# Transposed activations taken through DRAM by one write and one read, and two weight groups opened side by side at the start of a stage

## The chip, the cores and the metric

The kernel runs on one core of one Trainium2 chip. The metric is the device time of one execution in microseconds. Three runs of the kernel before lie within 0.1 us of each other.

## The reference

x has 256 rows (frames) of 1024 columns. Two layers do the same four things to it:

```python
h = rmsnorm(x, ffn1_norm[i]);  x = x + 0.5 * swiglu(h, w_gate, w_up, w_down)
h = rmsnorm(x, mix_norm[i]);   q_s, k_s, v_s, q_m = split(h @ w_in[i])
x = x + concat([self_attention(q_s, k_s, v_s), memory_attention(q_m, mem)]) @ w_out[i]
h = rmsnorm(x, ffn2_norm[i]);  x = x + 0.5 * swiglu(h, w_gate, w_up, w_down)
```

swiglu(h) is (silu(h @ w_gate) * (h @ w_up)) @ w_down with an inner width of 2816. Self-attention is chunked with a position bias in layer 0 and differential with rotary embedding in layer 1. All is f32 in DRAM.

## The kernel before, in words

The 256 rows are two blocks of 128, tb = 0 and 1. The stages follow one another: FFN, mixer, FFN, FFN, mixer, FFN. An FFN first goes through 11 groups of 256 inner columns (tile gu, gate and up side by side, one PSUM bank of 512 columns for each tb), then through 11 blocks of w_down (tile acc, four banks: tb by column half hf). A mixer has five projections of 512 columns (tile pj), attention, and an output projection (acc as well); the first mixer makes the memory's keys and values (tile kv) before its projections.

f32 precision comes from three products for each product: a weight is split into hi and lo, the activation into xh and xl, and `dense` (L376 to L393) issues hi with xh, lo with xh and hi with xl, each a matmul over 512 columns. The activation is the stationary operand, the weights stream.

Weights come in chunks of 1 MB (tile raw, three buffers, loaded by SP in the order of `add_chunk`). ScalarE casts a chunk to hi in four pieces (L302), VectorE subtracts to lo in four pieces (L314); hi and lo have four buffers each, and a buffer comes free when the last matmul with its chunk is done. In gu one chunk is one group and one half c of the 1024 rows, 12 matmuls for each tb.

The activations must stand transposed. After a stage `finish` (L460) adds the four acc banks to x, half by half: A = (tb 0, hf 0), B = (0, 1), C = (1, 0), D = (1, 1). `prep_half` (L417) turns the half by four TensorE transposes into a PSUM bank (tile xtp, L396), VectorE multiplies by the gain (y, L427), ScalarE casts to xh (L430), VectorE subtracts to xl (L432), and ScalarE later squares x for the norm (junk, L441). There are five such norms between stages: 1 to the first mixer, 2 to the second FFN, 3 to the third FFN, 4 to the second mixer, 5 to the last FFN. Half hf 0 feeds c = 0 of the next stage's first matmuls, hf 1 feeds c = 1. At the end of an FFN's down part the last three blocks are done for one acc bank after another (SPLIT, L554), so that the halves come one after another. A stage opens with group 0 alone: tb 0 c 0, tb 0 c 1, tb 1 c 0, tb 1 c 1.

The inner activation h of a group is evacuated by `evac` (L482): ScalarE makes sil (L491), VectorE h (L494) and four 128x128 block transposes (hb, L503), SP writes hb to DRAM (hd, L508) and reads it back by four DMAs of 32 partitions (hr, L514), and it is split into ht.

The order of every engine's queue is set by a planner in the program, the class Flow: it keeps an estimated time for each engine, lets the steps of all threads become due by estimates (3.0 us for the write and 4.0 us for the read of hd), and emits each instruction when it is due. On the chip each engine then works its queue off in that order and waits at the head of it.

## Time and profile before

| | us |
|---|---|
| Time, median of 3 runs (lowest, highest) | 974.91 (974.86, 974.94) |
| The profiled execution | 975.12 |
| Its span, first to last instruction | 973.3 |
| TensorE busy in the span | 964.6 |
| VectorE busy | 675.7 |
| ScalarE busy | 542.4 |

The profiled execution has 1.8 us outside its span and is 0.2 us above the median. The granted clock is 1.00 throughout. The profile counts a matmul as busy from its start to its modelled end, 0.39 us for 512 columns, while the next one starts 0.227 us later; so TensorE's real state is read from the distance of the starts and from the waits named in the timeline, not from its busy share.

### The profile page before, as it was taken

To read this page: it belongs to the slowest core of one execution; us is meant where nothing else is said; L and a number is where in the kernel's file an instruction comes from. 1 tells how busy PE (TensorE), PEld (TensorE's weight loads), DVE (VectorE), ACT (ScalarE), POOL (GpSimd) and SP (SyncE) were. 2 spreads that over 40 slices of the span, in tenths; PEclk is the share of its full clock that TensorE was granted. 3 is DMA by queue.
4 is the path that set the end of the run, shared out by engine and by line. 5 is a ranking of instruction groups with operands and counts; after the bars stand their busy time and mean duration, and the time that the engine had idled before them with its cause. 6 is when DMAs were issued, how large, how long until landed. Compare 5 with 4: busy or idle time off the path is not lost.

```text
span 973.3 us, 13393 instructions
## 1 busy us (share of the span) xinstructions
PE 964.6 (99%) x4576; PEld 791.3 (81%) x4576; DVE 675.7 (69%) x1485; ACT 542.4 (56%) x1159; POOL 60.1 (6%) x65
## 2 busy tenths in 40 slices
PE   9999999999999999999999999999999999999998
PEld 7888888887777888888888888888787788888886
DVE  6776675887777866666476676644989886676641
ACT  6554544766685655445445555443677764555540
POOL 0000000022210000000000000000344100000000
PEclk9999999999999999999999999999999999999999
DMA  9989766475525567887648887764641369788641
GB/s 289 306 242 270 257 225 206 162 260 173 174 87 173 163 209 223 242 263 242 235 124 252 250 252 237 253 207 136 207 140 50 125 199 284 235 251 254 226 130 44
DMA packets 164447, 200.90 MB, mean 206 GB/s; under 512 B 9433, under 2 KB 140058, under 8 KB 164378
## 3 DMA queue, kind: packets, MB, share of 16 engines
q1 hardware_dynamic: 164378, 200.04, 65.5%
q8 instruction: 36, 0.59, 0.3%
q14 instruction: 33, 0.27, 0.1%
HBM read 187.42 MB, written 12.58 MB: 205 GB/s over the span
## 4 chain that ended last, share of the span: by engine, by line
PE 91%; DVE 5%; ACT 1%; DMA 1%; issue 0%; SPq 0%; ACTq 0%
PE gu L383 16%; PE gu L386 16%; PE gu L389 16%; PE acc L386 9%; PE acc L389 9%; PE acc L383 9%; PE pj L389 3%; PE pj L383 3%; PE pj L386 3%; DVE lo L314 2%; PE xtp L396 1%; PE S L983 1%; PE AV L1064 1%; PE kv L389 1%; PE kv L386 1%; PE kv L383 1%
## 5 line engine op out<-in xcount | busy, mean ns | idle before, releaser
L314 DVE TENSOR_TENSOR lo<-raw,hi 128x512 fp32r<-128x512 f32 x656 | 416.5, 684 | 161.5 <-ACT hi L302 161.3
L302 ACT CAST hi<-raw 128x512 fp32r<-128x512 f32 x656 | 365.4, 618 | 241.3 <-PE gu L389 117.9
L389 PE MATMUL gu<-hi,xl 128*128 128x512 f32 x704 | 274.3, 390 | 0.0
L383 PE MATMUL gu<-hi,xh 128*128 128x512 f32 x704 | 274.1, 389 | 0.0
L386 PE MATMUL gu<-lo,xh 128*128 128x512 f32 x704 | 274.0, 389 | 0.0
L389 PEld LDWEIGHTS gu<-hi,xl 128*128 128x128 f32 x704 | 132.2, 188 | 27.5
L383 PEld LDWEIGHTS gu<-hi,xh 128*128 128x128 f32 x704 | 132.2, 188 | 27.3
L386 PEld LDWEIGHTS gu<-lo,xh 128*128 128x128 f32 x704 | 132.2, 188 | 27.2
L383 PE MATMUL acc<-hi,ht 128*128 128x512 f32 x352 | 137.7, 391 | 0.0
L386 PE MATMUL acc<-lo,ht 128*128 128x512 f32 x352 | 137.3, 390 | 0.2 <-DVE lo L314 0.2
L389 PE MATMUL acc<-hi,ht 128*128 128x512 f32 x352 | 137.4, 390 | 0.0
L386 PEld LDWEIGHTS acc<-lo,ht 128*128 128x128 f32 x352 | 66.1, 188 | 14.1 <-DVE lo L314 0.7
L389 PEld LDWEIGHTS acc<-hi,ht 128*128 128x128 f32 x352 | 66.1, 188 | 13.7
L383 PEld LDWEIGHTS acc<-hi,ht 128*128 128x128 f32 x352 | 66.1, 188 | 13.5
L523 DVE TENSOR_TENSOR ht<-hr,ht 128x512 fp32r<-128x512 f32 x44 | 30.3, 688 | 55.0 <-ACT ht L521 55.0
L521 ACT CAST ht<-hr 128x512 fp32r<-128x512 f32 x44 | 27.1, 617 | 69.5 <-DMA hr<-hd 69.5
L389 PE MATMUL pj<-hi,xl 128*128 128x512 f32 x160 | 64.6, 404 | 0.0
L386 PE MATMUL pj<-lo,xh 128*128 128x512 f32 x160 | 63.6, 398 | 0.0
L383 PE MATMUL pj<-hi,xh 128*128 128x512 f32 x160 | 63.6, 398 | 0.0
L491 ACT ACTIVATE sil<-gu,xr 128x256 f32<-128x256 f32 x88 | 41.4, 470 | 17.5 <-PE gu L389 17.5
L503 DVE STREAM_TRANSPOSE hb<-h 128x128 f32<-128x128 f32 x176 | 44.1, 289 | 1.2
L494 DVE SCALAR_TENSOR_TENSOR h<-gu,xr,sil 128x256 f32<-128x256 f32 x88 | 42.2, 480 | 1.6
(167 smaller groups left out, 806.5 us busy)
## 6 DMA issues: line engine op xcount, KB each, us to landing
raw<-in_ffn_w_down_dram SPq DMA_DIRECT2D x44, 1024.0 KB
raw<-in_ffn_w_gate_dram SPq DMA_DIRECT2D x86, 512.0 KB
raw<-in_ffn_w_up_dram SPq DMA_DIRECT2D x86, 512.0 KB
raw<-in_w_in_dram SPq DMA_DIRECT2D x32, 512.0 KB
hd<-hb SPq DMA_DIRECT2D x44, 256.0 KB
hr<-hd SPq DMA_DIRECT2D x176, 64.0 KB
raw<-in_w_out_dram SPq DMA_DIRECT2D x8, 1024.0 KB
raw<-in_w_mem_kv_dram SPq DMA_DIRECT2D x4, 1024.0 KB
```

The source lines that it names most:

```text
L302: nc.scalar.copy(out=c.hi[:, sl], in_=c.raw[:, sl])
L314: nc.vector.tensor_sub(c.lo[:, sl], c.raw[:, sl], c.hi.bitcast(F32)[:, sl])
L383: nc.tensor.matmul(out=ps, lhsT=xh, rhs=wh, start=start, stop=False)
L386: nc.tensor.matmul(out=ps, lhsT=xh, rhs=wl, start=False, stop=False)
L389: nc.tensor.matmul(out=ps, lhsT=xl, rhs=wh, start=False, stop=stop)
L396: nc.tensor.transpose(out=dst, in_=src, identity=flip if flipped else ident)
L491: nc.scalar.activation(sil, ps[tb][:, 0:256], AF.Silu, scale=xt.r[tb])
L494: nc.vector.scalar_tensor_tensor(out=h, in0=ps[tb][:, 256:512], scalar=xt.r[tb], in1=sil, op0=ALU.mult, op1=ALU.mult)
L503: nc.vector.transpose(out=hb[:, :, f, tb, :], in_=h[:, f * P:(f + 1) * P])
L521: nc.scalar.copy(out=hi, in_=src)
L523: nc.vector.tensor_sub(lo, src, hi.bitcast(F32))
L983: nc.tensor.matmul(out=ss[e][:, pr, :nk], lhsT=q[rows, pr, :], rhs=k[rows, pr, :], start=i == 0, stop=i == len(passes) - 1)
```

## The change

For a half marked `far`, prep_half makes no TensorE transposes: VectorE block-transposes x into xb, ScalarE's queue issues a DMA that writes xb to DRAM (xd) and then one that reads it back into 128 partitions with the blocks in place (xr); the gain is multiplied from xr, and the rest is as before. At norms 1, 3 and 4 all four halves are far, at norms 2 and 5 only C and D. The planner waits 4.2 us after the write and 5.6 us after the read.

The inner h goes by one block transpose of 256 columns for each tb, one write and one read of 128 partitions. Every FFN but the first opens with groups 0 and 1 side by side: tb 0 with c 0 of both, c 1 of both, then tb 1; the second mixer does so with projections 0 and 1. The weights are loaded in that order. The last down blocks before norms 3 and 4 are four in place of three.

```diff
@@ -336,15 +336,15 @@
     WO = (0, 1, 2, 3)
 
     def plan_ffn(l, nm, wg, wu, wd):
...
+        gu = [[None, None] for _ in range(NG)]
+        order = [(g, c) for g in range(NG) for c in range(2)]
+        if (l, nm) != (0, 1):
+            order[1:3] = order[2:0:-1]
+        for g, c in order:
+            pieces = 2 if len(chunks) < 2 else 1
+            a = cols4(wg[l], c, g * 256, 256, 0, pieces)
+            b = cols4(wu[l], c, g * 256, 256, 256, pieces)
+            gu[g][c] = add_chunk([q for ab in zip(a, b) for q in ab])
...
@@ -360,16 +360,16 @@
...
+        order = [(i, c) for i in range(len(WI)) for c in range(2)]
+        if l % 2 == 1:
+            order[1:3] = order[2:0:-1]
...
@@ -414,18 +414,41 @@
             self.rt = [None, None]
             self.done = [0, 0]
 
-    def prep_half(xt, tb, hf, gc, wait=0.0):
-        yield banks.has()
-        tp = bank("xtp")
-        for k in range(4):
-            t = turn(tp[:, k, :], xs[tb][:, hf * 512 + k * P:hf * 512 + (k + 1) * P])
-        yield t
-        yield g2.has()
-        y = g2.take([P, 4, P], F32, "y")
+    def prep_half(xt, tb, hf, gc, wait=0.0, far=False):
         ks = slice(hf * 4, hf * 4 + 4)
         g = gcol[:, gc + hf * 4:gc + hf * 4 + 4]
-        nc.vector.tensor_tensor(out=y, in0=tp, in1=g.unsqueeze(2).broadcast_to([P, 4, P]), op=ALU.mult)
-        banks.give()
+        if far:
+            yield g2.has(2)
+            xb = g2.take([P, 4, 4, 32], F32, "xb")
+            nc.vector.transpose(out=xb.rearrange("p b k j -> p k b j"),
+                                in_=xs[tb][:, hf * 512:(hf + 1) * 512].rearrange("p (k i b) -> p k b i", k=4, b=4))
+            yield flow.dve(512, 0.3)
+            d = dram.tile([4, 32, 4, P], F32, tag="hd", name="xd")
+            nc.scalar.dma_start(out=d.rearrange("a i b x -> (a i) (b x)"), in_=xb.rearrange("p b k j -> p (b k j)"))
+            flow.act(0, 0.25)
+            yield flow.now + 4.2
+            g2.give()
+            yield g2.has()
+            xr = g2.take([P, 4, P], F32, "xr")
+            nc.scalar.dma_start(out=xr, in_=d.rearrange("a i b x -> (i b) a x"))
+            flow.act(0, 0.25)
+            yield flow.now + 5.6
+            yield g2.has()
+            y = g2.take([P, 4, P], F32, "y")
+            nc.vector.tensor_tensor(out=y.rearrange("p k (a j) -> p k a j", a=4),
+                                    in0=xr.rearrange("p a (k j) -> p k a j", k=4),
+                                    in1=g.unsqueeze(2).unsqueeze(3).broadcast_to([P, 4, 4, 32]), op=ALU.mult)
+            g2.give()
+        else:
+            yield banks.has()
+            tp = bank("xtp")
+            for k in range(4):
+                t = turn(tp[:, k, :], xs[tb][:, hf * 512 + k * P:hf * 512 + (k + 1) * P])
+            yield t
+            yield g2.has()
+            y = g2.take([P, 4, P], F32, "y")
+            nc.vector.tensor_tensor(out=y, in0=tp, in1=g.unsqueeze(2).broadcast_to([P, 4, P]), op=ALU.mult)
+            banks.give()
         yield flow.dve(512)
         nc.scalar.copy(out=xt.h[tb][:, ks, :], in_=y)
@@ -472,7 +495,10 @@
...
-                yield from prep_half(xt, tb, hf, gc)
+                if far and hf == 0:
+                    flow.spawn(prep_half(xt, tb, hf, gc, far=True))
+                else:
+                    yield from prep_half(xt, tb, hf, gc, far=far)
@@ -499,24 +525,22 @@
                 if hb is None:
                     hb = g2.take([P, 4, 2, 2, 32], F32, "hb")
                 yield t
-                for f in range(2):
-                    nc.vector.transpose(out=hb[:, :, f, tb, :], in_=h[:, f * P:(f + 1) * P])
-                    t = flow.dve(128, 0.05)
+                nc.vector.transpose(out=hb[:, :, tb].rearrange("p b f j -> p f b j"),
+                                    in_=h.rearrange("p (f i b) -> p f b i", f=2, b=4))
+                t = flow.dve(256, 0.05)
                 g2.give()
+            yield t
             hd = dram.tile([4, 32, 4, P], F32, tag="hd", name="hd")
-            yield t
-            nc.sync.dma_start(out=hd.rearrange("a i b x -> (a i) (b x)"), in_=hb.rearrange("p b f t j -> p (b f t j)"))
+            nc.sync.dma_start(out=hd.rearrange("a i b x -> (a i) (b x)"), in_=hb.rearrange("p b t f j -> p (b t f j)"))
             yield flow.now + 3.0
             g2.give()
             yield g2.has()
-            hr = g2.take([P, 4, 2, 2, 32], F32, "hr")
-            for b in range(4):
-                nc.sync.dma_start(out=hr[32 * b:32 * b + 32].rearrange("p a f t j -> p a (f t j)"),
-                                  in_=hd[:, :, b, :].rearrange("a i x -> i a x"))
+            hr = g2.take([P, 4, P], F32, "hr")
+            nc.sync.dma_start(out=hr, in_=hd.rearrange("a i b x -> (i b) a x"))
             yield flow.now + 4.0
             yield g4.has()
             ht = g4.take([P, 2, 4, P], F32R, "ht")
-            src = hr.rearrange("p a f t j -> p (f t) a j")
+            src = hr.rearrange("p a (c j) -> p c a j", c=4)
             hi, lo = (ht[:, i].rearrange("p c (a j) -> p c a j", a=4) for i in range(2))
             nc.scalar.copy(out=hi, in_=src)
             yield flow.act(512)
@@ -525,20 +549,36 @@
...
-            order = [(tb, c) for tb in range(2) for c in range(2)] if g == 0 and (l, nm) != (0, 1) else \
-                    [(tb, c) for c in range(2) for tb in range(2)]
...
+        rest = 0
+        if (l, nm) != (0, 1):
+            grps = []
+            for tb in range(2):
+                for c in range(2):
+                    for g in range(2):
+                        if tb == c == 0:
+                            grps.append(open_group(g))
+                        run(grps[g], tb, c)
+            rest = 2
+        for g in range(rest, NG):
+            grp = open_group(g)
+            for c in range(2):
+                for tb in range(2):
+                    run(grp, tb, c)
...
-        SPLIT = NG - 3
+        SPLIT = NG - 4 if nm == 2 and gc_next is not None or l == 1 and nm == 1 else NG - 3
@@ -563,9 +603,14 @@
         if nm == 1:
             table_hint(AF.Exp)
         for tb in range(2):
-            flow.spawn(finish(acc, tb, nxt, gc_next, True))
+            flow.spawn(finish(acc, tb, nxt, gc_next, True, nxt is not None))
+            first = SPLIT if tb == 0 or SPLIT == NG - 3 else NG - 2
+            for c in range(SPLIT, first):
+                for k in range(2):
+                    for hf in range(2):
+                        down(c, k, tb, hf)
             for hf in range(2):
-                for c in range(SPLIT, NG):
+                for c in range(first, NG):
                     for k in range(2):
                         t = down(c, k, tb, hf)
                 acc.t[tb][hf] = t
@@ -846,16 +891,20 @@
...
+        def proj(*parts):
+            pss = []
             for tb in range(2):
                 for c in range(2):
...
+                    for n, (i, evac) in enumerate(parts):
+                        if tb == c == 0:
+                            flow.until(banks.has(2))
+                            pss.append([bank(f"pj{j}", (P, 512)) for j in range(2)])
...
@@ -1202,13 +1251,18 @@
                 memory_kv(ll)
         for c, tb in ((0, 0), (0, 1), (1, 0), (1, 1), (2, 0), (3, 0), (2, 1), (3, 1)):
             flow.spawn(unit(c, tb))
-        proj(0, qk_evac(0))
-        flow.until(g4.has(2))
-        take_v()
-        proj(1, v_evac)
-        proj(2, qk_evac(1))
-        proj(3, qk_evac(2))
-        proj(4, vq_evac)
+        if typ_a:
+            proj((0, qk_evac(0)))
+            flow.until(g4.has(2))
+            take_v()
+            proj((1, v_evac))
+        else:
+            flow.until(g4.has(3))
+            take_v()
+            proj((0, qk_evac(0)), (1, v_evac))
+        proj((2, qk_evac(1)))
+        proj((3, qk_evac(2)))
+        proj((4, vq_evac))
-            flow.spawn(finish(acc, tb, nxt, gc_next, False))
+            flow.spawn(finish(acc, tb, nxt, gc_next, False, tb == 1))
```

TensorE has 24 groups of four transposes of x before and 8 after; those left are the four at the program's start and A and B of norms 2 and 5.

ScalarE at norm 3, before, in the opening of the third FFN: hi are weights, xh_4484 is the activation of tb 1 (here its half D), gu_4932 the first group of tb 0.

```order
L302 CAST hi_4959<-raw_4820 128x512 x3
L430 CAST xh_4484<-y 128x512
L302 CAST hi_4959<-raw_4820 128x512
L491 ACTIVATE sil<-gu_4932,xr 128x256
L441 ACTIVATE junk,xss<-x_86 128x512
L302 CAST hi_5020<-raw_4942 128x512 x4
```

The cast of D stands ahead of the first sil. After, at the same place (xh_4383 is tb 0, xh_4384 is tb 1; gu_4818 and gu_4847 are groups 0 and 1 of tb 0):

```order
L302 CAST hi_4825<-raw_4770 128x512 x3
L427 DMA xd<-xb 128x512
L302 CAST hi_4825<-raw_4770 128x512
L453 CAST xh_4383<-y 128x512
L464 ACTIVATE junk,xss<-x_85 128x512
L433 DMA xr<-xd 128x4x128 x2
L517 ACTIVATE sil<-gu_4818,xr 128x256
L517 ACTIVATE sil<-gu_4847,xr 128x256
L453 CAST xh_4384<-y 128x512
L464 ACTIVATE junk,xss<-x_86 128x512
L453 CAST xh_4384<-y 128x512
```

The casts of C and D have moved behind both sil of tb 0, and two writes and two reads stand among the casts.

VectorE at norm 3, before, up to the first h (xl_4486 is tb 1):

```order
L427 TENSOR_TENSOR y<-xtp,gcol 128x512
L314 TENSOR_TENSOR lo_4925<-raw_4783,hi_4924 128x512 x2
L314 TENSOR_TENSOR lo_4960<-raw_4820,hi_4959 128x512 x2
L432 TENSOR_TENSOR xl_4486<-y,xh_4484 128x512
L314 TENSOR_TENSOR lo_4960<-raw_4820,hi_4959 128x512
L494 SCALAR_TENSOR_TENSOR h<-gu_4932,xr,sil 128x256
```

After, from the first h on (xl_4386 is tb 1):

```order
L520 SCALAR_TENSOR_TENSOR h<-gu_4818,xr,sil 128x256
L528 STREAM_TRANSPOSE hb<-h 128x2x4x32
L438 TENSOR_TENSOR y<-xr,gcol 128x512
L520 SCALAR_TENSOR_TENSOR h<-gu_4847,xr,sil 128x256
L438 TENSOR_TENSOR y<-xr,gcol 128x512
L455 TENSOR_TENSOR xl_4386<-y,xh_4384 128x512
```

The subtraction for C has moved behind the h of both groups and behind the products of C and D.

ScalarE at norm 4, before, in the opening of the second mixer (xh_6035 is tb 1, sq is the square of projection 0, tb 0):

```order
L302 CAST hi_6470<-raw_6334 128x512 x2
L302 CAST hi_6503<-raw_6378 128x512 x4
L430 CAST xh_6035<-y 128x512
L583 ACTIVATE sq<-pj_6485,xr 128x512
L441 ACTIVATE junk,xss<-x_86 128x512
L302 CAST hi_6566<-raw_6482 128x512 x4
```

And after (xh_5883 is tb 0, xh_5884 is tb 1; V is made from projection 1, tb 0):

```order
L453 CAST xh_5883<-y 128x512
L464 ACTIVATE junk,xss<-x_85 128x512
L433 DMA xr<-xd 128x4x128 x2
L628 ACTIVATE sq<-pj_6319,xr 128x512
L453 CAST xh_5884<-y 128x512
L979 ACTIVATE V_6317<-pj_6348,xr 128x512
L464 ACTIVATE junk,xss<-x_86 128x512
L453 CAST xh_5884<-y 128x512
```

Here the cast of C stands behind the sq of projection 0 alone, and ahead of V.

More of the change, by code (lines that the diff above doesn't have):

```diff
@@ L458, in __init__, with finish @@
             self.t = [[None, None], [None, None]]
-    def finish(acc, tb, xt, gc, half):
+    def finish(acc, tb, xt, gc, half, far):
         for hf in range(2):
@@ L526, in evac, with open_group, run @@
             hts[g], htt[g] = ht, t
-        for g, ids in enumerate(plan[l, nm, "gu"]):
+        def open_group(g):
             flow.until(banks.has(2))
-            ps = [bank(f"gu{tb}", (P, 512)) for tb in range(2)]
-            end = [None, None]
+            ps, end = [bank(f"gu{tb}", (P, 512)) for tb in range(2)], [None, None]
             flow.spawn(evac(g, ps, end))
-            order = [(tb, c) for tb in range(2) for c in range(2)] if g == 0 and (l, nm) != (0, 1) else \
-                    [(tb, c) for c in range(2) for tb in range(2)]
-            for tb, c in order:
-                for k in range(4):
-                    kk = 4 * c + k
-                    t = dense(ps[tb], xt.h[tb][:, kk, :], xt.l[tb][:, kk, :], lambda: xt.t[tb][kk], ids[c], k,
-                              lambda w: k4(w)[:, k, :], kk == 0, kk == KT - 1)
-                if c == 1:
-                    end[tb] = t
+            return g, ps, end
+        def run(grp, tb, c):
+            g, ps, end = grp
+            for k in range(4):
+                kk = 4 * c + k
+                t = dense(ps[tb], xt.h[tb][:, kk, :], xt.l[tb][:, kk, :], lambda: xt.t[tb][kk],
+                          plan[l, nm, "gu"][g][c], k, lambda w: k4(w)[:, k, :], kk == 0, kk == KT - 1)
+            if c == 1:
+                end[tb] = t
+        rest = 0
[13 more added lines that the diff above has]
+                    run(grp, tb, c)
         flow.until(banks.has(4))
```

42 lines of the change are left out of this document (14 added, 28 removed).

## The prediction

> **What bounds the kernel now.** I read the page's busy times and chain first.
>
> ```profile
> span 973.3 us, 13393 instructions
> ...
> PE 964.6 (99%) x4576; PEld 791.3 (81%) x4576; DVE 675.7 (69%) x1485; ACT 542.4 (56%) x1159; POOL 60.1 (6%) x65
> ...
> PE 91%; DVE 5%; ACT 1%; DMA 1%; issue 0%; SPq 0%; ACTq 0%
> ```
>
> TensorE bounds it: 91% of the chain is its own work, and VectorE and ScalarE have slack on the average. So an edit counts only if it takes instructions from TensorE or makes it wait. What TensorE's instructions cost stands in its timeline at norm 3, where one group of transposes sits between matmuls.
>
> ```profile
> 479.71 0.39 PE L383 MATMUL acc<-hi,ht 128*128 128x512 f32 x1
> ...
> 489.91 0.60 PE L396 MATMUL xtp<-ident,x 128*128 128x128 f32 x4
> ...
> 492.67 0.39 PE L386 MATMUL acc<-lo,ht 128*128 128x512 f32 x1
> ```
>
> From 479.71 to 489.91 there are 45 starts: 10.20 / 45 = 0.2267 us for a matmul. From 489.91 to 492.67 are 2.76 us with ten matmuls beside the group; ten take 2.27, so the group of four costs 0.49 us.
>
> **What is removed.** 16 of the 24 groups go (four halves at norms 1, 3, 4, two at 2 and 5): 16 x 0.49 = 7.84 us, all on the bound. Everything below asks how much of it waiting takes back.
>
> **What the handover is made of.** Call E the start of a stage's first matmul. Four blocks of 12 matmuls (tb 0: c 0 of both groups, c 1 of both) come before tb 1 in the changed opening, so C is wanted at Z = E + 48 x 0.2267 = E + 10.88, B at E + 5.44; the product with xl is the third, 0.45 later. The steps from x to xl, by operation (count | busy, mean ns | idle):
>
> ```profile
> L427 DVE TENSOR_TENSOR y<-xtp,gcol 128x512 f32<-128x512 f32 x24 | 16.5, 689 | 15.8 <-PE xtp L396 15.8
> L430 ACT CAST xh<-y 128x512 fp32r<-128x512 f32 x24 | 14.8, 618 | 33.6 <-DVE y L427 33.6
> L432 DVE TENSOR_TENSOR xl<-y,xh 128x512 fp32r<-128x512 f32 x24 | 16.5, 688 | 4.8 <-ACT xh L430 4.5
> L466 DVE SCALAR_TENSOR_TENSOR x<-acc,x 128x512 f32<-128x512 f32 x16 | 11.0, 690 | 20.0 <-PE acc L389 20.0
> ```
>
> And how closely engines follow each other, from the timeline at the opening of the third FFN and at two other places:
>
> ```profile
> 491.27 0.62 ACT L430 CAST xh<-y 128x512 fp32r<-128x512 f32 x1 [4.42 <-DVE y L427]
> 491.93 0.69 DVE L432 TENSOR_TENSOR xl<-y,xh 128x512 fp32r<-128x512 f32 x1 [0.69 <-ACT xh L430]
> ...
> 507.92 0.39 PE L389 MATMUL gu<-hi,xl 128*128 128x512 f32 x1
> ...
> 508.41 0.47 ACT L491 ACTIVATE sil<-gu,xr 128x256 f32<-128x256 f32 x1 [1.17 <-PE gu L389]
> ...
> 508.69 0.69 DVE L314 TENSOR_TENSOR lo<-raw,hi 128x512 fp32r<-128x512 f32 x1
> 508.78 0.62 ACT L441 ACTIVATE junk<-x 128x512 bf16<-128x512 f32 x1
> ...
> 509.30 0.48 DVE L494 SCALAR_TENSOR_TENSOR h<-gu,xr,sil 128x256 f32<-128x256 f32 x1
> 509.69 0.15 DVE L450 TENSOR_TENSOR sst<-xss 128x1 f32<-128x1 f32 x1
> ...
> 757.84 0.48 DVE L971 SCALAR_TENSOR_TENSOR oT<-otp,gcs,oT 128x256 fp32r<-128x256 f32 x1
> ...
> 758.37 0.49 PE L383 MATMUL acc<-hi,oT 128*128 128x512 f32 x1 [0.44 <-DVE oT L971]
> ```
>
> The last matmul of a tb starts at 507.92 and the slot after it at 508.15; sil starts at 508.41, so 0.26 after the slot. ScalarE's next instruction starts 0.37 after sil; VectorE's next starts 0.60 after one of 512 columns (508.69 to 509.30) and 0.39 after an h; xl starts 0.66 after its cast does; a stopped TensorE runs on 0.05 after VectorE's end (758.32 to 758.37) and its first matmul is 0.10 longer (0.49), 0.15 in all.
>
> **Added: a wait at norms 2, 3 and 5.** At norm 3 the cast of C stands behind the sil of group 1, tb 0, and that needs the last matmul before Z. At norms 2 and 5 ScalarE's order is the same. So however early C's data is there, sil starts at Z + 0.26, the cast runs from 0.63 to 1.25, and TensorE, which wants xl at Z + 0.45, must stand. VectorE then has h of group 1 at about Z + 0.78 (sil's end and a little), and its next at Z + 1.17. At norm 3 the product y of D stands there (0.60), so xl runs 1.77 to 2.46 and TensorE goes on at 2.61: 2.61 - 0.45 = 2.15 us. At norm 5 the block transpose hb of 256 columns stands there in place of y. Its row is not in the trace; the nearest:
>
> ```profile
> L503 DVE STREAM_TRANSPOSE hb<-h 128x128 f32<-128x128 f32 x176 | 44.1, 289 | 1.2
> L491 ACT ACTIVATE sil<-gu,xr 128x256 f32<-128x256 f32 x88 | 41.4, 470 | 17.5 <-PE gu L389 17.5
> L494 DVE SCALAR_TENSOR_TENSOR h<-gu,xr,sil 128x256 f32<-128x256 f32 x88 | 42.2, 480 | 1.6
> ```
>
> One of 128 takes 0.29, so the step is between 0.29 and 0.58; as for h (0.48, step 0.39) I take 0.35 to 0.4: 1.9 us. At norm 2 a short rotary step (0.15, like the sst above) comes too: 2.05. The lower bound of each is VectorE free: xl from 1.29 to 1.98, 1.7 us. The upper bound is a late read, below. Sum 6.1 us (5.1 at least). Nothing covers these: TensorE's queue has no other work ahead of tb 1.
>
> **Norm 4.** The cast of C stands behind the sq of projection 0, tb 0, only, and projection 0 ends 12 matmuls before Z.
>
> ```profile
> L583 ACT ACTIVATE sq<-pj,xr 128x512 f32<-128x512 f32 x12 | 8.2, 688 | 1.4 <-PE pj L389 1.4
> L586 DVE TENSOR_REDUCE hss<-sq 128x8 f32<-128x512 f32 x12 | 8.2, 680 | 1.4 <-ACT sq L583 1.4
> ```
>
> From E: 36 matmuls 8.16, sq from 8.42 to 9.11, on VectorE hss to about 9.8 and a short step, C's y from 10.0 to 10.7, cast to 11.35, xl to 12.1; wanted at 11.33, with the restart 0.9 us. It is 0 if y gets ahead of hss, and about 2 if D's steps get ahead. I take 0.9.
>
> **The way through DRAM.** No x goes that way before, but h does, in blocks of the same size; SP's issues (start, time of the issue) and the casts that take the data:
>
> ```profile
> 351.36 1.88 SPq L514 DMA_DIRECT2D hr<-hd  x4
> ...
> 358.71 0.62 ACT L521 CAST ht<-hr 128x512 fp32r<-128x512 f32 x1 [3.57 <-DMA hr<-hd]
> ...
> 518.15 0.51 SPq L270 DMA_DIRECT2D raw<-in_ffn_w_up_dram  x1
> 518.71 0.50 SPq L508 DMA_DIRECT2D hd<-hb  x1
> 524.09 2.43 SPq L514 DMA_DIRECT2D hr<-hd  x4
> ...
> 528.18 0.62 ACT L521 CAST ht<-hr 128x512 fp32r<-128x512 f32 x1 [1.96 <-DMA hr<-hd]
> ...
> 869.59 0.34 SPq L508 DMA_DIRECT2D hd<-hb  x1
> 871.79 1.39 SPq L514 DMA_DIRECT2D hr<-hd  x3
> ```
>
> A write takes 869.59 to 871.79 = 2.2 us, and 518.71 to 524.09 = 5.4 right behind a weight chunk. A read takes 524.09 to 528.18 = 4.1 and 351.36 to 358.71 = 7.35 at the outside. One read of 128 partitions in place of four of 32 is not in the trace; I take 4.1 to 5, near the shorter, since the issues of the four alone are 1.9 to 2.4 us of it. C's read is issued about E + 5 to E + 5.9 by ScalarE's order, so C lies in SBUF at E + 9.1 to E + 10.9 and needs y (0.69) by Z + 0.63: in time, by a little.
>
> The Trainium skill, in "DMA: Bandwidth & Descriptors" under "Issuing engines are not separate DMA queues", speaks against the queue of ScalarE's own: DMAs of all issuers share 16 engines and interleave, so only issuing time is saved. The write that took 5.4 us behind a weight chunk agrees that the load decides.
>
> **B at norms 3 and 4.** Before B's second step ScalarE has eight weight casts, a square and two DMA issues to do.
>
> ```profile
> 502.47 3.73 ACT L302 CAST hi<-raw 128x512 fp32r<-128x512 f32 x7
> ```
>
> That is 0.53 us a cast. From E - 1.1, where TensorE sets the buffers free, 8 x 0.53 + 0.63 + two issues (0.34 to 0.5 each, as SP's above) and the cast and xl of B end about E + 5.9, when B is wanted (E + 5.89). I take 0.1 each, 0.2 in sum (0 to 1).
>
> **Costed at nothing.** The 16 block transposes of x (estimate 0.7 to 1.2 us each, two to four times the 0.29 row) and the 88 of h in place of 176 (together some 13 us less of VectorE) lie on an engine 69% busy, in the slack ahead of each handover; without that cover each would cost about its time. One issue in place of four frees SP, which bounds nothing (0% of the chain). The 32 DMA issues on ScalarE wait at its head for the write; behind them are queued weight casts that mostly wait for TensorE's buffers. If that cover fails, lo comes late for TensorE by the write's excess, which is in the slower rival. Norm 1 has the memory's keys and values, 96 matmuls (21.8 us), in front of it: no gap. Four split blocks add no matmul.
>
> **Sum.** -7.84 + 6.1 + 0.9 + 0.2 = -0.64 us. The profiled execution took 975.12 (span 973.3 and 1.8 around it), 0.21 above the median; against the median 974.91 the sum gives 974.3 us.
>
> **Rivals.**
>
> *Faster.* The gaps are at their lower bound (5.1 + 0.9), and the second mixer, where TensorE waits already, gives its waits back because two projections now open it side by side.
>
> ```profile
> 686.00:786.00 100.00, 97.82 (x551) 77.56 (x550) 90.47 (x200) 68.87 (x191) 30.89 (x27) 1.00 0.46 149
> ```
>
> In these 100 us (the second mixer; busy time of TensorE, its loads, VectorE, ScalarE, GpSimd; granted clock; DMA share) TensorE lacks 2.2 us. The sum is -7.84 + 6.0 - 2.2 = -4.0: 970.9. For it: the removal is certain, and a more relaxed DVE helps there. Against it: VectorE is busy 90.47 of 100 there, so it may not be able to give.
>
> *Slower, by late reads.* C and D come at the outside time of the row, 7.35 us. The point from which it decides is a read over about 5.5 us at C. C then lands some 2 us later, and gaps become 3.9 at norms 3 and 4 and 2.9 at 2 and 5: 13.6 against 7.84 removed, with B's 0.2 about +6: 980.9. For it speaks the load just there:
>
> ```profile
> 510.00:520.00 10.00, 10.00 (x46) 8.29 (x45) 6.94 (x16) 5.51 (x11) 0.86 (x1) 1.00 0.92 286
> ```
>
> The DMA engines were 92% busy right after the opening of the third FFN, and the interleaved opening brings four chunks at that time. Against it: the reads of h meet the same load, and most took nearer to 4 us.
>
> In the Trainium skill, "TensorE: Matmul & The Clock Gate", "What's actually happening", an idle window of about 3.4 us halves TensorE's clock until it has been busy as long; by an estimate from that page, each such gap would lose 1.7 us more, some 984 in all. The granted clock is 1.00 throughout here, so no run yet shows it.
>
> *Slower, in the second mixer.* tb 0's first projection is done at E + 8.2 in place of E + 5.4, tb 1's at about 19 in place of 10.9, so attention starts 3 to 8 us later, and VectorE with its 90% can't catch up. If TensorE waits 3.2 us there, the sum is +2.6: 977.5. It decides from more wait than 2.6 us in that stage.
>
> *That it does not do what it says:* TensorE's order has the 16 groups gone, so that is no case of its own.
>
> **How the numbers follow.** The forecast, the waits taking back nearly all, has 0.43; faster 0.32; late reads 0.12; the second mixer 0.13. About 0.2% (1.95 us) is what a measurement of this kernel can tell from no change, so the forecast's own range, 972.9 to 976.5 by the bounds above, lies mostly in "same". From the cases: faster 0.34, same 0.42, slower 0.24. The range that leaves out no more than 2 in 10 goes from a little under the faster rival, 970.5, to above the mixer's one, 979.0; most of the late reads stay outside.
>
> **What would show it.** 8 groups xtp instead of 24 on TensorE; a stop of TensorE at its first product with xl of tb 1 near 2 us at norms 2, 3 and 5, released by VectorE's xl, whose cast began right behind a sil; about 0.9 at norm 4, none at norm 1. If those stops are under 1 us, the order argument is wrong; if ScalarE's idle before the cast or VectorE's before y ends by xr, the reads are late; if the second mixer's TensorE lacks more or less than 2.2 us per 100, a rival on it holds.

## The result and the profile after

The changed kernel takes 988.31 us (median of 4 runs, 986.29 to 990.69) against 974.88 for the kernel before on the same chip: a ratio of 1.0136 [1.0123, 1.0149], 13.4 us slower. The prediction said 974.3, with a range of 970.5 to 979.0. The profiled execution is the lowest of the four: 986.29 us, span 984.5. The page, its busy times and chain:

```profile
span 984.5 us, 12955 instructions
...
PE 963.2 (98%) x4512; PEld 786.0 (80%) x4512; DVE 701.3 (71%) x1413; ACT 543.1 (55%) x1159; POOL 61.0 (6%) x65
...
PE 86%; DMA 5%; DVE 5%; ACT 2%; POOL 0%; issue 0%; SPq 0%; ACTq 0%
PE gu L389 16%; PE gu L386 16%; PE gu L383 16%; PE acc L383 9%; PE acc L389 9%; PE acc L386 9%; DMA xd<-xb 3%; PE pj L383 2%; PE pj L389 2%; PE pj L386 2%; DMA xr<-xd 2%; PE S L1032 1%; PE AV L1113 1%; DVE lo L314 1%; PE ptp L396 1%; ACT hi L302 1%
```

DMA had 1% of the chain and has 5%: the write of xb and the read of xd stand on it. VectorE's work has grown, by 25.6 us. What TensorE waits for (line waited for: us in all, times, longest):

```profile
PE gu L383 <- ACT xh L453: 4.1, 3, 1.9
PE xtp L396 <- DMA x<-in_x_dram: 3.3, 1, 3.3
PE gu L389 <- DVE xl L455: 1.8, 4, 0.6
PE AV L1170 <- ACT PT L1046: 1.6, 1, 1.6
PE pj L383 <- ACT xh L453: 1.4, 1, 1.4
...
PE kmtp L396 <- DVE kmn L637: 1.1, 1, 1.1
PE qktp L396 <- DVE m L938: 0.9, 2, 0.6
PE pj L389 <- DVE xl L455: 0.5, 1, 0.5
```

The stops that were forecast are there (gu and pj, for xh and xl), and beside them one at the memory's keys (kmtp, norm 1) and some in the second mixer's attention (qktp, AV).

To put them in place I divide each profile at the first matmul of every stage and compare the stages' lengths with those of the kernel before. This table is worked out from the traces, in us of the profiled execution; "down" is the three down parts ahead of norms 1, 3 and 4, "mixer 1" includes the memory's keys and values, "rest" is the start, the first FFN's groups and the end. Medians are over all runs but two that stood far off, one of 1966 us in e2 and one of 1067 us in e5.

| kernel | down | mixer 1 | FFN 2 gu | FFN 3 gu | mixer 2 | FFN 4 gu | rest | span | median (before) |
|---|---|---|---|---|---|---|---|---|---|
| after | -4.3 | +0.3 | +1.7 | +4.5 | +4.3 | +3.3 | +1.4 | +11.2 | 988.31 (974.88) |
| e1 | -4.3 | +3.9 | +0.5 | +4.1 | +2.7 | +0.4 | +1.7 | +9.0 | 982.27 (975.32) |
| e2 | -0.1 | 0.0 | 0.0 | 0.0 | -1.9 | 0.0 | +2.2 | +0.3 | 973.86 (975.32) |
| e3 | 0.0 | 0.0 | 0.0 | 0.0 | -0.7 | 0.0 | -0.3 | -1.1 | 974.79 (975.32) |
| e4 | -1.4 | +2.1 | 0.0 | 0.0 | -0.7 | 0.0 | -0.1 | -0.2 | 975.30 (975.32) |
| e5 | -4.4 | +0.7 | +0.5 | +1.3 | +3.1 | +0.4 | +0.2 | +1.9 | 977.84 (975.23) |
| e6 | -4.4 | -0.9 | +0.6 | +1.2 | +3.1 | +0.7 | +0.2 | +0.4 | 975.62 (975.23) |
| e7 | -4.4 | +1.1 | +1.7 | +2.5 | +4.8 | +1.7 | +2.3 | +9.8 | 983.96 (975.23) |
| e8 | -2.0 | +1.8 | 0.0 | 0.0 | -1.5 | 0.0 | -0.2 | -1.9 | 973.39 (975.23) |
| e9 | -4.4 | -0.9 | +0.5 | +0.4 | +2.2 | +0.7 | +0.4 | -1.1 | 974.02 (974.89) |
| e10 | -0.1 | 0.0 | 0.0 | 0.0 | -1.8 | 0.0 | +0.4 | -1.5 | 973.58 (974.89) |
| e11 | -1.5 | +1.2 | 0.0 | 0.0 | -0.7 | 0.0 | +0.6 | -0.3 | 974.51 (974.89) |
| e12 | -1.0 | 0.0 | 0.0 | 0.0 | -1.8 | 0.0 | +0.5 | -2.3 | 972.70 (974.89) |

A stage that loses nothing would show minus 0.49 for each group of transposes that it no longer holds: one each in mixer 1's memory stage and in its output projection, one in FFN 2, one in FFN 3, two in mixer 2, one in FFN 4. "Rest" has nothing to do with the change after the first FFN's start: the first matmul comes at 8.6 to 11.0 us in these profiles, by when x arrives, and the first FFN's opening is the same code in all. e2 and e7 have besides 1.4 us of half speed there.

Where the time goes in the changed kernel is best seen at norm 3. ScalarE's rows there (start, length; ACTq are its DMA issues):

```profile
503.67 0.34 ACTq L427 DMA_DIRECT2D xd<-xb  x1
...
509.53 1.30 ACTq L433 DMA_DIRECT2D xr<-xd  x2
512.14 0.47 ACT L517 ACTIVATE sil<-gu,xr 128x256 f32<-128x256 f32 x1 [4.14 <-PE gu L389]
514.80 0.47 ACT L517 ACTIVATE sil<-gu,xr 128x256 f32<-128x256 f32 x1 [2.18 <-PE gu L389]
516.03 0.62 ACT L453 CAST xh<-y 128x512 fp32r<-128x512 f32 x1 [0.75 <-DVE y L438]
```

VectorE's product for C, in the same view:

```profile
515.30 0.69 DVE L438 TENSOR_TENSOR y<-xr,gcol 128x512 f32<-128x512 f32 x1 [1.49 <-DMA xr<-xd]
```

And TensorE:

```profile
514.38 0.39 PE L389 MATMUL gu<-hi,xl 128*128 128x512 f32 x1
516.70 0.50 PE L383 MATMUL gu<-hi,xh 128*128 128x512 f32 x1 [1.93 <-ACT xh L453]
517.04 0.40 PE L386 MATMUL gu<-lo,xh 128*128 128x512 f32 x1
517.64 0.80 PE L389 MATMUL gu<-hi,xl 128*128 128x512 f32 x1 [0.20 <-DVE xl L455]
518.24 0.63 PE L383 MATMUL gu<-hi,xh 128*128 128x512 f32 x1
518.66 0.63 PE L386 MATMUL gu<-lo,xh 128*128 128x512 f32 x1
```

C's write was issued at 503.67 and its read at 509.53, 5.9 us later; the read landed at 515.30, 5.8 us later. The sil of group 1 was at 514.80, so here both reasons meet: by the order alone the cast could have come at 515.17 (514.80 and 0.37), the data moved it to 516.03. TensorE stood 1.93 us. Then something that the sum did not hold: from 518.24 on the matmuls are 0.42 us apart in place of 0.227. The windows of that stretch (busy times; then granted clock, DMA share, GB/s) say why:

```profile
512.00:516.00 4.00, 2.76 (x13) 1.95 (x11) 1.82 (x4) 0.95 (x2) 0.00 (x0) 1.00 1.09 329
516.00:520.00 4.00, 3.10 (x8) 2.17 (x9) 2.94 (x7) 2.38 (x6) 0.55 (x1) 0.66 0.46 148
```

The granted clock was 0.66 in the four us behind the stop: TensorE ran at half speed for part of them. The DMA engines were full while C's read was under way.

At norm 2 C's data was early, and the order alone is seen. ScalarE, then TensorE:

```profile
332.25 0.47 ACT L517 ACTIVATE sil<-gu,xr 128x256 f32<-128x256 f32 x1 [2.18 <-PE gu L389]
332.62 0.61 ACT L453 CAST xh<-y 128x512 fp32r<-128x512 f32 x1
```

```profile
331.82 0.39 PE L389 MATMUL gu<-hi,xl 128*128 128x512 f32 x1
333.28 0.50 PE L383 MATMUL gu<-hi,xh 128*128 128x512 f32 x1 [1.07 <-ACT xh L453]
...
334.54 0.50 PE L389 MATMUL gu<-hi,xl 128*128 128x512 f32 x1 [0.52 <-DVE xl L455]
```

The sil starts, the cast follows 0.37 later, and TensorE's starts are 1.46 and (333.62 to 334.54) 0.92 apart in place of 0.23 each: 1.9 us in all, as the sum had it, with no half clock behind.

At norm 5 TensorE stops twice in the same way, and there half speed follows:

```profile
809.46 0.50 PE L383 MATMUL gu<-hi,xh 128*128 128x512 f32 x1 [1.07 <-ACT xh L453]
...
810.72 0.72 PE L389 MATMUL gu<-hi,xl 128*128 128x512 f32 x1 [0.53 <-DVE xl L455]
811.24 0.63 PE L383 MATMUL gu<-hi,xh 128*128 128x512 f32 x1
```

The windows tell the two places apart. I lay them so that one begins where the half speed does, first at norm 5, then at norm 2:

```profile
807.42:810.83 3.41, 1.81 (x8) 0.87 (x6) 2.44 (x6) 1.60 (x4) 0.00 (x0) 1.00 1.10 344
810.83:814.24 3.41, 3.41 (x9) 2.64 (x10) 1.38 (x4) 1.24 (x3) 0.56 (x1) 0.50 0.29 91
...
329.55:332.96 3.41, 2.66 (x12) 1.88 (x10) 2.13 (x6) 1.19 (x3) 0.00 (x0) 1.00 1.05 338
332.96:336.37 3.41, 2.56 (x10) 1.83 (x11) 3.05 (x9) 2.00 (x6) 0.00 (x0) 1.00 0.45 148
```

The half speed at norm 5 lasts from 810.83 to 814.24, 3.41 us at a clock of 0.50; at norm 3 it lasts as long, from 517.28. The two begin 293.55 us apart, 86 times 3.413, and the two of e1 below (from 210.07 and 520.69) 91 times. This fits windows of 3.413 us on a fixed grid. On that grid both stops of norm 5 lie in one window, while at norm 2 a border, 332.96, falls between them and each window keeps more of its work (2.66 and 2.56 us in place of 1.81).

### The profile page after: what moved, and what is told of

Same layout as the page of the kernel before. It is cut to its first block, busy times and chain, and to the rows that moved or that the text cites. A ratio compares the mean times of both kernels' runs of the same rounds, so it can differ in the third digit from the quotient of the medians.

```text
span 984.5 us, 12955 instructions
## 1 busy us (share of the span) xinstructions
PE 963.2 (98%) x4512; PEld 786.0 (80%) x4512; DVE 701.3 (71%) x1413; ACT 543.1 (55%) x1159; POOL 61.0 (6%) x65
## 4 chain that ended last, share of the span: by engine, by line
PE 86%; DMA 5%; DVE 5%; ACT 2%; POOL 0%; issue 0%; SPq 0%; ACTq 0%
PE gu L389 16%; PE gu L386 16%; PE gu L383 16%; PE acc L383 9%; PE acc L389 9%; PE acc L386 9%; DMA xd<-xb 3%; PE pj L383 2%; PE pj L389 2%; PE pj L386 2%; DMA xr<-xd 2%; PE S L1032 1%; PE AV L1113 1%; DVE lo L314 1%; PE ptp L396 1%; ACT hi L302 1%
## 5 line engine op out<-in xcount | busy, mean ns | idle before, releaser
L528 DVE STREAM_TRANSPOSE hb<-h 128x256 f32<-128x256 f32 x88 | 55.7, 632 | 1.2
```

The costliest lines, as they stand in the source:

```text
L528: nc.vector.transpose(out=hb[:, :, tb].rearrange("p b f j -> p f b j"), in_=h.rearrange("p (f i b) -> p f b i", f=2, b=4))
```

## The experiments

All times are medians; the ratio is that of the runs of one call with its 95% interval. Four theories are told apart: the **order** (C's cast behind the sil of group 1), the **data** (writes and reads under load are late), the **clock** (half speed behind a stop), and the **queue** (other work behind an engine that stands for the data).

**e1: the cast ahead of the sil.** In `evac`, tb 0 of group 1 in an opening:

```diff
                 yield end[tb]
+                if rest and g == 1 and tb == 0:
+                    yield lambda: xt.t[1][0] is not None
...
```

> The changed kernel, with one thing moved: at norms 2, 3 and 5 ScalarE's cast of C stands ahead of the sil of group 1, tb 0. Order theory (the stop before tb 1 comes from that sil): norm 2 falls from 1.9 to about 0.95 us and norm 5 from 2.2 to 0.85, by where y of C ends in the changed kernel's trace, and with the shorter stop the half clock behind norm 5 (1.6 us) goes: about 984.4 us against 988.3. Norm 3 stays, since there C's read lands only after the sil. Late-read theory (the data is what is late everywhere): all stops stay, 988.3.

Measured: 982.27 us, ratio 1.0063 [1.0043, 1.0082]. FFN 2 falls from +1.7 to +0.5, FFN 4 from +3.3 to +0.4 with its half clock gone, FFN 3 stays (+4.1): the order theory, as told, and at norm 3 the data theory. The median fell 6.0 us, more than the 3.9 expected, though this profile had a worse stop at the memory's keys than the changed kernel's. Its row, and two of the matmuls behind it, show the data and the queue at work at norm 1:

```profile
208.66 0.44 PE L396 MATMUL kmtp<-ident,kmn 128*128 128x128 f32 x2 [3.00 <-DVE kmn L638]
...
210.53 0.63 PE L386 MATMUL kv<-lo,memh 128*128 128x512 f32 x1
210.96 0.63 PE L389 MATMUL kv<-hi,meml 128*128 128x512 f32 x1
```

A stop of 3.0 us, and half speed behind it (0.43 us apart). VectorE in the same kernel:

```profile
207.23 0.69 DVE L438 TENSOR_TENSOR y<-xr,gcol 128x512 f32<-128x512 f32 x1 [2.08 <-DMA xr<-xd]
...
208.12 0.48 DVE L638 SCALAR_TENSOR_TENSOR kmn<-kv,mr,hf 128x256 f32<-128x256 f32 x1
```

VectorE stands 2.08 us at C's product for the read; kmn, the normalisation of the keys, is queued right behind, and TensorE needs it.

**e2: no x through DRAM.** Both `finish` calls get False for `far`; openings, split blocks and h stay.

```diff
-            flow.spawn(finish(acc, tb, nxt, gc_next, True, nxt is not None))
+            flow.spawn(finish(acc, tb, nxt, gc_next, True, False))
...
-            flow.spawn(finish(acc, tb, nxt, gc_next, False, tb == 1))
+            flow.spawn(finish(acc, tb, nxt, gc_next, False, False))
```

> The changed kernel with all transposes of x on TensorE again; openings side by side, four split blocks and the new way of h stay. If the way of x through DRAM makes the stops (14.5 us at the five norms in the profile of the changed kernel), they go and 7.8 us of transposes come back: about 981.7 us, with the 3.0 us lost in the second mixer and the 1.6 us at the start still there. If the openings or the new way of h make the stops: 988.3 + 7.8 = 996. If everything lost hangs on x through DRAM, mixer included: 977.

Measured: 973.86 us, ratio 0.9983 [0.9971, 0.9994]. Lower than every forecast: with the transposes back on TensorE (7.8 us of work) the kernel is 14.4 us below the changed one. All that is lost hangs on the way of x through DRAM, the second mixer included, which gains 1.9 us.

**e3: the new h alone**, in the kernel before.

```diff
-                for f in range(2):
-                    nc.vector.transpose(out=hb[:, :, f, tb, :], in_=h[:, f * P:(f + 1) * P])
+                nc.vector.transpose(out=hb[:, :, tb].rearrange("p b f j -> p f b j"),
...
-            for b in range(4):
-                nc.sync.dma_start(out=hr[32 * b:32 * b + 32].rearrange("p a f t j -> p a (f t j)"),
+            nc.sync.dma_start(out=hr, in_=hd.rearrange("a i b x -> (i b) a x"))
...
```

> The kernel before, with only the new way of h (one block transpose of 256 columns for each tb, one write, one read of 128 partitions). The prediction costed it at nothing: 974.9 within 1 us. Rival: the wider transposes and the single read delay weights or h, and part of the 13.4 us is theirs: 977 or more.

Measured: 974.79 us, ratio 0.9994 [0.9983, 1.0005]: no change in time, as costed. The profile has 0.75 us less in the second mixer.

**e4: the new h, and x through DRAM at norm 1 only**, old openings.

```diff
-            flow.spawn(finish(acc, tb, nxt, gc_next, True))
+            flow.spawn(finish(acc, tb, nxt, gc_next, True, l == 0 and nm == 1))
...
```

> The kernel before, with the new way of h and with x through DRAM at norm 1 alone (old openings, three split blocks). Four groups gone are 1.96 us. If the price there is the 1.2 us that the first mixer's memory keys wait in the changed kernel's profile: 974.1. If norm 1 is free: 972.9. If ScalarE's waits at the DMAs delay more: over 975.5.

Measured: 975.30 us, ratio 1.0001 [0.9990, 1.0011], between the 974.1 of the first case and the 975.5 of the last. The down part gives 1.4 (three groups) and the first mixer loses 2.1 where 0.49 should go. TensorE's waits:

```profile
PE kmtp L396 <- DVE kmn L637: 2.2, 2, 1.6
```

Norm 1 is not free, and the keys are the place.

**e5: nobody waits for the data.** e1, with the product from x itself, which leaves out the transposition:

```diff
-                                    in0=xr.rearrange("p a (k j) -> p k a j", k=4),
+                                    in0=xs[tb][:, hf * 512:(hf + 1) * 512].rearrange("p (a k j) -> p k a j", a=4, k=4),
```

> e1 with the gain multiplied from x itself instead of from what was read back: transposes, writes, reads and their order stay, only nobody waits for the data (this leaves out the transposition of x in 16 halves). Late-read theory for what is left after e1 (norm 1 where VectorE stands at C's y with the memory's keys queued behind it, norm 3 and norm 4 at C): these stops and the half clock after them go, only B's stop at norms 3 and 4 (0.7 each, xl behind four weight subtractions) stays: 976 to 978 against 982.3. If ScalarE's standing at the writes or the traffic is what costs: stays near 982.

Measured: 977.84 us, ratio 1.0029 [1.0015, 1.0043], 4.4 below e1 and in the band. FFN 3 falls from +4.1 to +1.3 and mixer 1 from +3.9 to +0.7: the data theory at norms 1 and 3. Mixer 2 does not fall (+3.1, of which 0.95 is half speed behind its AV stop that e1's profile does not have). In mixer 1 a stop of 1.6 at later keys is left, and it has another cause. ScalarE's casts of weights there, with the square for these keys queued behind them:

```profile
217.56 1.14 ACT L302 CAST hi<-raw 128x512 fp32r<-128x512 f32 x2 [2.74 <-DMA raw<-in_w_in_dram]
```

They wait 2.74 us for a weight chunk.

**e6: no DMA either.** e5 without the two `dma_start` of `prep_half`; it leaves out the transposition too.

```diff
-            nc.scalar.dma_start(out=d.rearrange("a i b x -> (a i) (b x)"), in_=xb.rearrange("p b k j -> p (b k j)"))
...
-            nc.scalar.dma_start(out=xr, in_=d.rearrange("a i b x -> (i b) a x"))
```

> e5 without the 32 DMAs (the block transposes stay; this leaves out the transposition of x in 16 halves and its way through DRAM). If waiting for the data was all: the same as e5 within 1 us. If ScalarE's standing at its queue's head for the writes, or the 8.4 MB of traffic, cost beside it: 2 us or more below e5.

Measured: 975.62 us, ratio 1.0007 [0.9998, 1.0016]: 2.2 below e5, just over the 2 us that was set for it, from only four runs of e5 between 976.4 and 980.0. The spans of the two profiles differ by 1.4 us, and the stages show it in mixer 1 (+0.7 to -0.9). The casts that stood for the weight chunk begin at 215.31 in place of 217.56, and the stop at the later keys is gone. SP issued those weights at 209.34 in place of 209.94, so about 0.6 us of it is from what came before, and the rest points to the DMA engines' load: from 192 to 208 their share is 0.66, then 0.75 here, and 1.01, then 1.07 in e5. That is for norm 1 alone. The more telling number is the level: with no transposes of x on TensorE and no DMA for it, the kernel is still no faster than before. The order of what is left, and VectorE's block transposes (e9), with the stops and half speed they bring, take all 7.8 us back.

**e7: idle matmuls in the stops.** The changed kernel, nine matmuls ahead of tb 1's first in each opening:

```diff
+        def fill(ps, xh, c):
+            for _ in range(9):
+                nc.tensor.matmul(out=ps, lhsT=xh, rhs=k4(c.hi)[:, 0, :], start=True, stop=True)
...
+                        if tb == 1 and c == g == 0:
+                            fill(grps[0][1][1], xt.h[0][:, 0, :], plan[l, nm, "gu"][0][0])
...
```

> The changed kernel with nine idle matmuls (9 x 0.227 = 2.0 us, into a bank that the next matmul starts afresh) on TensorE in the four stops before tb 1 at norms 2 to 5. They take the place of standing, so they cost about nothing there. Clock theory (the half clock behind norms 3 and 5 comes from the stop): it goes, 3.4 us in the profiled execution: 984 to 985 against 988.3. If the half clock has another cause, or its time is not on the end: 988.3 to 989.

Measured: 983.96 us, ratio 1.0088 [1.0066, 1.0110], 4.3 below the changed kernel with 8.2 us more of TensorE work (36 matmuls). FFN 3 falls from +4.5 to +2.5, FFN 4 from +3.3 to +1.7. The windows at norm 3 of this kernel, which hold the nine and what follows:

```profile
514.00:518.00 4.00, 4.00 (x19) 3.32 (x18) 2.74 (x6) 1.66 (x4) 0.00 (x0) 1.00 1.13 324
518.00:522.00 4.00, 4.00 (x19) 3.17 (x18) 2.05 (x7) 2.17 (x7) 0.55 (x1) 1.00 0.37 116
```

Granted clock 1.00 where the changed kernel had 0.66, and no half speed at norm 5 either: the clock theory holds. Work that does nothing made the kernel faster.

**e8: x through DRAM where the half has time**: `far` by half, A and B at norm 1, A at norms 3 and 4.

```diff
+            flow.spawn(finish(acc, tb, nxt, gc_next, True, (tb == 0, tb == 0 and l == 0 and nm == 1)))
...
+            flow.spawn(finish(acc, tb, nxt, gc_next, False, (False, False)))
...
```

> The changed kernel with x through DRAM only where the half has time: A and B at norm 1, A at norms 3 and 4; all else by TensorE as in e2. If the way through DRAM pays where nobody waits for it: four groups, 1.96 us, below e2: about 972. If it costs by its mere work on VectorE and ScalarE: 974 or more.

Measured: 973.39 us, ratio 0.9994 [0.9983, 1.0004]. A miss by 1.4: norms 3 and 4 give 0.5 each, but mixer 1 loses 1.8, though C and D don't go through DRAM. TensorE stops 1.7 us at the first keys, and ahead of them VectorE stood at A's product this time:

```profile
196.84 0.69 DVE L438 TENSOR_TENSOR y<-xr,gcol 128x512 f32<-128x512 f32 x1 [2.25 <-DMA xr<-xd]
```

**e9: e6 without the block transposes of x**, all else in the same order (the transposition is left out here too).

```diff
-            nc.vector.transpose(out=xb.rearrange("p b k j -> p k b j"),
...
             yield flow.dve(512, 0.3)
```

> e6 without the 16 block transposes of x, all other instructions in the same order (it leaves out the transposition of x in 16 halves). In e6 the second mixer still loses 4.9 us against e2. If VectorE's 1.1 us for each transpose is what makes that stage late: 4 us or more below e6, 971 to 972. If it is the order (the casts and subtractions of C and D behind the first projections' work): within 1 us of e6, 975.

Measured: 974.02 us, ratio 0.9993 [0.9980, 1.0007], 1.6 below e6: between the two, nearer the order. Mixer 2 keeps +2.2 where e2 has -1.9. Its stops are those of the changed kernel:

```profile
PE AV L1166 <- ACT PT L1042: 1.6, 1, 1.6
PE qktp L396 <- DVE m L934: 0.9, 2, 0.6
```

By the table VectorE's extra work is worth 0.8 us of the 4.9 between e6 and e2 there. But this profile has a window of half speed behind the AV stop (738.12 to 741.53, granted clock 0.50), which e6's does not have: from that stop to the output projection e9 and e5, which has it too, take 16.4 us, e6 and e1 15.4. Without it VectorE's work would be worth 1.8. The other 3.1, by elimination, go to the order of the second mixer with C's and D's steps among the first projections'. Which of its instructions decides was not tried.

**e10: the second mixer opened by two projections, alone** (e3 with that).

```diff
-            proj((0, qk_evac(0)))
-            flow.until(g4.has(2))
+            flow.until(g4.has(3))
             take_v()
-            proj((1, v_evac))
+            proj((0, qk_evac(0)), (1, v_evac))
...
```

> e3 (the kernel before with the new way of h) with the second mixer opened by two projections side by side, nothing else. If e2's gain (1.9 us in the second mixer's stages) comes from that opening: 973.7 against e3's 974.8, since e3 has 0.75 of it by itself. If from the FFN openings or the fourth split block: 974.8.

Measured: 973.58 us, ratio 0.9986 [0.9977, 0.9995]. Mixer 2 is at -1.8 as in e2, and at -0.7 in e3, so the opening is worth 1.1 us and the new h the rest. In the stages it is 4.5 us less in the projections and 3.4 more in the output projection than in e3.

**e11: e4 with longer planned times at norm 1.**

```diff
-            yield flow.now + 4.2
+            yield flow.now + 7.0
...
-            yield flow.now + 5.6
+            yield flow.now + 7.0
```

> e4 with the planned times of write and read at norm 1 set to 7.0 us each in place of 4.2 and 5.6, so that C's product stands behind the memory keys' normalisation in VectorE's queue. Queue theory (VectorE stands at the head for the read, the keys stand behind it, TensorE waits for the keys): e4's 2.1 us of loss in the memory and first projection stages go: 973.2 against 975.3. If the keys are late by VectorE's work: 975.3.

Measured: 974.51 us, ratio 0.9994 [0.9985, 1.0003], 0.8 below e4 in place of 2.1. The stop at the first keys is gone (1.76 to 0.21 us between TensorE's starts), but one of 1.4 comes at later keys:

```profile
PE kmtp L396 <- DVE kmn L637: 1.2, 1, 1.2
```

The queue theory holds for the place it was made for. The later stop does not come from x's data. VectorE's row for those keys, and what GpSimd (POOL), which makes hf, had to do first:

```profile
217.13 0.48 DVE L637 SCALAR_TENSOR_TENSOR kmn<-kv,mr,hf 128x256 f32<-128x256 f32 x1 [1.87 <-POOL hf L403]
...
215.70 0.31 POOL L887 MEMSET bias<- 64x256 f32 x1 [5.54 <-ACT hi L302]
```

GpSimd stood 5.54 us at a memset, with hf queued behind it: the same kind of wait, on a third engine.

**e12: A at norms 3 and 4 only.**

```diff
+            flow.spawn(finish(acc, tb, nxt, gc_next, True, (tb == 0 and (l, nm) != (0, 1), False)))
...
```

> e8 without the way through DRAM at norm 1: only A at norms 3 and 4 goes through DRAM. In e8's profile the keys of the memory wait 1.8 us at norm 1 for 0.99 saved, so 0.8 below e8: 972.6, and about 2.5 below the kernel before. If e8's gain is not from norms 3 and 4: 973.9 as e2.

Measured: 972.70 us, ratio 0.9972 [0.9962, 0.9982]: the fastest of all, 2.2 below the kernel before, of which 1.0 is from two groups of transposes and the rest from the second mixer (its opening and the new h). Its chain:

```profile
PE 94%; DVE 4%; DMA 1%; ACT 1%; issue 0%; POOL 0%; SPq 0%; POOLq 0%; DVEq 0%
```

## Why the prediction was wrong

**What bounds it, and what is removed: right.** The three down parts gave 1.43 to 1.45 us each for three groups, 0.48 a group.

**The stops at norms 2 and 5: right in mechanism and size.** 1.9 us measured at norm 2 (2.05 forecast) and the same at norm 5 (1.9), from the starts of TensorE's matmuls; e1 moved the cast, and about 1 us was left at each, as expected. At norm 5 the block transpose of 256 columns was taken as a step of 0.35 to 0.4. Its step is 0.56 (809.46 to xl at 810.02), near the upper bound of 0.58 that the text gave. Its row:

```profile
L528 DVE STREAM_TRANSPOSE hb<-h 128x256 f32<-128x256 f32 x88 | 55.7, 632 | 1.2
```

So VectorE did not save 13 us by it: it spends 55.7 us on these in place of 44.1.

**The price of a stop: the step that failed most plainly.** The sum took a stop at its own length. Behind norm 3 and norm 5 TensorE then ran at half speed, about 1.6 us each in the profiled execution, and e7 got 4.3 us of the median back by filling the stops. The prediction had half speed only beside the late reads, from a sentence of the Trainium skill ("TensorE: Matmul & The Clock Gate", "What's actually happening": an idle window of about 3.4 us). The same section says that the window runs freely. The trace agrees with that, by the grid above, and disagrees with reading the rule as a bound on one stop: the stop at norm 3 was 1.93 us, with a short one of 0.2 behind it, and of two like pairs (1.07 and 0.5 with two matmuls between) the one at norm 5 had half speed behind it and the one at norm 2 had not. What the runs bear out is that 2 us of stops can cost it when they fall into one window. How much idle time in a window is enough does not come out of these traces: a window of e7 with 1.6 us of TensorE's work (from 204.69) had no half speed behind it, one of e1 with 1.9 (from 517.27) had. This also goes with the scatter of the changed kernel (986.3 to 990.7): its three other runs had a mean granted clock of 0.993, the profiled one, the shortest, 0.997.

**The way through DRAM: "in time, by a little" was wrong.** C's read was to be issued at E + 5 to E + 5.9 by ScalarE's order and to take 4.1 to 5, so that C lay in SBUF by E + 10.9. The write had no term of its own there, though a row of 5.4 us stood beside that of 2.2. At norm 3 (E = 502.86) the read could only go out when the write had landed, 5.9 us after its issue, at E + 6.7, and took 5.8 itself: C was there at E + 12.4, 1.5 us behind the bound. The medians by issue (count, KB, us to landing):

```profile
hd<-hb SPq DMA_DIRECT2D x44, 256.0 KB, 2.1
hr<-hd SPq DMA_DIRECT2D x44, 256.0 KB, 5.0
...
xd<-xb ACTq DMA_DIRECT2D x16, 256.0 KB, 3.7
xr<-xd ACTq DMA_DIRECT2D x16, 256.0 KB, 4.5
```

The 3.7 lies between two groups. Of the sixteen writes of x the trace has the landing of six: three took 2.0 us, with the DMA engines' share at 0.32 to 0.34 meanwhile, and three took 5.3 to 6.6, with a share of 0.81 to 1.01. So the load decides, and at the handover the opening's weights come. The late-reads rival had the mechanism, and its turning point, a read of over 5.5 us at C, was passed at norm 3; but it put the late data at norms 2 to 5, and they decide at norms 1, 3 and 4. At norm 4 the stop at C was 1.6 in place of 0.9; VectorE waited 1.0 of it for the read. B's stops at norms 3 and 4 were 0.7 each in place of 0.1, there with the data in time: four weight subtractions stood ahead of B's xl.

**Norm 1 "no gap": wrong.** It was argued from TensorE's 96 matmuls of cover alone. The text named what is queued behind the waiting reads on ScalarE, and not what is queued behind the waiting product on VectorE: the keys' normalisation. The keys' stops are 1.2 us in the changed kernel, 3.2 and half speed in e1's profile, 1.8 in e4's, where 0.8 more come later behind a weight chunk.

**The second mixer: both rivals were half right.** The opening does gain (e10: 1.1 us), and C's and D's late steps lose it again and more (e9, e2): mixer 2 is at +4.3 where e2 has -1.9. The sum had nothing for this. About 2.3 of these 6.2 us are the stops at B and C; the transposes gone there should have given 1.0.

**The account** of the profiled execution: 7.8 us saved; stops with half speed 1.9 at norm 2 (2.05 forecast), 4.9 at norm 3 (2.25 with B's), 2.3 at norm 4 (1.0 with B's), 3.7 at norm 5 (1.9), 1.2 at norm 1 (none), 3.0 more in mixer 2 (none), and 1.6 at the start, which is not the change's; that is 10.8 of the 11.2 us by which the span grew. The other 2.2 us of the medians' distance are not in a profile. By an estimate they are more half speed: one window of 3.41 us at 0.50 lowers the mean clock of 985 us by 0.0017, so 0.993 in place of 0.997 would be two windows more.

**What stays open:** which instruction in the second mixer makes its attention late, how much idle time in a window brings half speed, and whether the load or ScalarE's standing for the writes costs anything beyond norm 1.

## What to carry to other kernels

When a step moves from the busiest engine to a DMA, its data get a latency at the moment of the heaviest load: list, for every in-order engine that will stand for it, the consumer's too, what is queued behind, and give the move only to pieces that have the time (here one half in four, at two of five norms). Price a stop of the matrix engine with the half speed that can follow it, and take a transfer's time from the row at the same load. An order in which a cast stands behind the work of the stage it feeds costs its time even when the data are early (1.9 us at norm 2), and can be read off before anything runs.

## What the runs showed of the hardware

- Half speed of TensorE came in windows of 3.41 us at a granted clock of 0.50 (starts 0.42 to 0.43 us apart), which began whole multiples of 3.413 us from each other: 86 between norms 3 and 5, 91 in e1. It followed a stop of 1.9 us and one of 3.0 us. Two stops of 1.07 and 0.53 us inside one such window were followed by it, the like pair with a border between was not. Nine matmuls that compute nothing, put into the stops, prevented it (e7).
- A write of 256 KB took 2.0 us to landing where the DMA engines' share was 0.32 to 0.34, and 5.3 to 6.6 us where it was 0.81 to 1.01.
- One block transpose on VectorE of 128x256 takes 632 ns, against 289 for each of 128x128: nothing is saved by joining them. One of 128x512 takes 1.09 us.
- One read of 128 partitions has a median of 5.0 us to landing; it is not clearly shorter than the four of 32 partitions, and e3 shows no gain by it.
